# The first gate block of an encoder kernel from 32-bit products of unscaled rows, their norm applied behind

## The chip, the cores and the metric

The kernel runs on one core of a Trainium2 chip. The time is that of one execution on the device in microseconds, the median of several runs. TensorE (PE) multiplies, VectorE (DVE), ScalarE (ACT) and GpSimd (POOL) work on rows, and SyncE (SP) issues the DMAs. Each engine takes its instructions in the order in which they stand in its own queue.

## The reference

Two layers of an encoder over 2048 rows of 1024 numbers. Cut to what matters here:

```python
for l in range(DEPTH):                       # DEPTH = 2
    h = rmsnorm(x, pre_g[l])                 # x / sqrt(mean(x*x) + eps) * pre_g
    proj = h @ w_in[l]                       # (2048, 1024) @ (1024, 2816)
    u_a, v_a, g_a, q, k, v, g_b = split(proj)
    y_a = gmlp_group(u_a, v_a, ...) * silu(g_a)
    y_b = gqa_axial_attention(q, k, v, ...) * silu(g_b)      # g_b: 512 columns
    x = x + rmsnorm(concat(y_a, y_b) @ w_out[l], post_g[l])
```

The change concerns g_b of the first 512 rows in the first layer.

## The kernel before

The rows are worked on in four groups of 512 (`GRP`), each of four row blocks of 128. For a group, `hT_jobs` makes `hT`, the normalised rows turned so that the 1024 columns lie on the partitions, in two 16-bit halves: `load` brings a row block `x_t`, `squares` sums its squares on ACT, a chain of small steps on DVE (`chain`, `chain_two`; tiles `rs`, `rr`) makes the inverse norm, `scale` multiplies the left half of the row on ACT and the right half on POOL, `turn` transposes four 128x128 blocks on PE into a PSUM tile `pt` (a bundle, below), `high` casts that to the upper 16-bit half on ACT and `low` subtracts on DVE for the lower half. A weight block of 256 columns, `w_raw`, is split likewise by `split_steps`: maxima and a small product `pe` over all partitions give a power of two, then eight pieces are made into 16-bit halves `w_hl` (upper on ACT, lower on DVE), each multiplied by the gain `g_col` on the way. `proj_tok` then multiplies one row block by one weight block in three passes of eight 16-bit products (upper by upper, upper by lower, lower by upper), and `do_gb` makes the gate from two such results: tanh on ACT, one step on DVE, a store to `gb_d`.

The order of blocks begins with the two gate blocks `gb0` and `gb1` for group 0, then for groups 1, 2 and 3, then keys and the rest. Other work is hung into a block by `bg`, a list of jobs with due times: a `tick` comes after every pass of eight products, and jobs whose tick has come are issued there, at most four at a time. A gate block has 12 ticks, so the gates of group 1 start at tick 24, those of group 2 at tick 48. `start(g + 1)` hangs the next group's squares, norms and transposes in; for group 2 the transposes come at ticks 38 to 45. Engines named `PE`, `ACT`, `DVE`, `POOL` in capitals keep the program's order (`Pinned`, whose line 89 is that of nearly all instructions in the profile); the others are placed by the scheduler of the build.

Group 0 is opened by hand, at the end of the program: the first row block is loaded, squared, scaled, turned and split, the first weight is measured by squares on ACT (`sums=4`) and split on ACT, DVE and POOL, and the rest follows through `bg`:

```python
    z = jobs.chain(0)
    steps[1]()
    jobs.scale(0, z)
    steps[2]()
    banks = [jobs.turn(0, 0)]
...
    for d in range(ND):
        w.high(d, d % 2 == 1)
...
    for n, f in enumerate(steps2):
        bg.add((5, 5, 8, 9, 10, 10, 10, 10, 11, 11, 11, 11, 11)[n], f)
```

PSUM has eight banks for all tiles of `ps_t`; a tile's bank is taken again when its last reader is done.

Of the kernel before, what the change touches and what calls it, by code (L numbers as in the profile page):

```python
# [9 lines left out]
F32 = mybir.dt.float32  # L10
# [4 lines left out]
ALU = mybir.AluOpType  # L15
# [4 lines left out]
P = 128  # L20
# [23 lines left out]
def encoder(ctx: ExitStack, tc, x, w_in, w_out, pre_g, post_g, ln_a_g, ln_a_b,  # L44
# [19 lines left out]
    def big_t(shape, name, dt=F32R):  # L64
        return big.tile(shape, dt, name=name, tag="big")
# [4 lines left out]
    def f_t(name, n=GRP, dt=F32):  # L70
        return fp.tile([P, n], dt, name=name, tag="f")
# [4 lines left out]
    def ps_t(name):  # L76
        return psum.tile([P, GRP], F32, name=name, tag="ps", bufs=8)
# [66 lines left out]
            f()  # L144
        return z

    def rsqrt_rows_steps(parts, v, eps):

        n = parts.shape[1]
        m, z, t = [small.tile([P, n], F32, name=f"rr_{i}", bufs=2) for i in range(3)]  # L150
# [50 lines left out]
    class Project:  # L201
# [22 lines left out]
        def begin(self):  # L224

            self.w_first = [Obj(), Obj()]
            steps = []
# [123 lines left out]
        def split_steps(self, w, raw, act=ACT, dve=DVE, sums=0):  # L351

            w.ready = False
            col = small.tile([P, 32], F32, name="w_col", bufs=5)
# [2 lines left out]

            def part(i):
                sl = slice(i * ND // 2, (i + 1) * ND // 2)
                if i == 0 and sums:  # L360
                    def f():
                        for d in range(sums):
                            junk = f_t("fb")
                            act.activation(junk[:, 0:WB], raw[:, d], AF.Square, scale=self.g_col[:, d:d + 1],
                                           accum_out=col[:, 18 + d:19 + d])
                    return f
                return lambda: dve.tensor_reduce(top[:, sl], raw[:, sl], AX.X, ALU.max, apply_absolute_value=True)

            def square():
                ds8 = slice(sums, ND)  # L370
                dve.tensor_tensor(top[:, ds8], top[:, ds8], self.g_col[:, ds8], ALU.mult)
                dve.tensor_reduce(sq, top[:, ds8], AX.X, ALU.max, apply_absolute_value=True)
                if sums:
                    dve.tensor_reduce(inv, col[:, 18:18 + sums], AX.X, ALU.add)
                    dve.tensor_scalar(sq, sq, sq, inv, ALU.mult, ALU.add)
                    dve.tensor_scalar(sq, sq, W_SPREAD, None, ALU.mult)
                else:
                    dve.tensor_scalar(sq, sq, sq, W_SPREAD, ALU.mult, ALU.mult)

            def scale():  # L380
                ps = ps_t("pe")
                PE.matmul(ps[:, 0:1], ones, sq, start=True, stop=True)
                ei = w.e.bitcast(I32)
                dve.tensor_scalar(ei, ps[:, 0:1].bitcast(I32), -0.5, RSQRT_MAGIC, ALU.mult, ALU.add)
                dve.tensor_scalar(ei, ei, EXP_BITS, None, ALU.bitwise_and)
                dve.tensor_scalar(ei, ei, float(87 << 23), float(187 << 23), ALU.max, ALU.min)
                dve.tensor_scalar(w.eg, self.g_col, w.e, None, ALU.mult)

            def high(d, on_dve=False):
                if d == 0:  # L390
                    w.hl = w_t([P, 2, ND, WB], "w_hl", F16)
                if on_dve:
                    dve.tensor_scalar(w.hl[:, 0, d], raw[:, d], w.eg[:, d:d + 1], None, ALU.mult)
                    return
                act.activation(w.hl[:, 0, d], raw[:, d], AF.Copy, scale=w.eg[:, d:d + 1])

            def low(d, lo=None):
                if lo:
                    scaled = f_t("fb")[:, 0:WB]
                    lo.tensor_scalar(scaled, raw[:, d], w.eg[:, d:d + 1], None, ALU.mult)  # L400
                    lo.tensor_tensor(w.hl[:, 1, d], scaled, w.hl[:, 0, d], ALU.subtract)
                    return
# [32 lines left out]
        def hT_jobs(self, g):  # L435
# [61 lines left out]
            def trans(j, q):  # L497
# [43 lines left out]
        def norm_rope(self, banks, n, tb, eps):  # L541
# [10 lines left out]
            for i, src in enumerate(banks):  # L552
# [204 lines left out]
        def run(self, kv, first, last_jobs, first_wo):  # L757
# [168 lines left out]
    def attend(l, kv, nxt):  # L926
# [587 lines left out]
    jobs.squares(0)
    for j in range(1, TPG):
        jobs.load(j, ACT)
    steps[0]()
    z = jobs.chain(0)
    steps[1]()
    jobs.scale(0, z)  # L1520
    steps[2]()
    banks = [jobs.turn(0, 0)]
    jobs.squares(1)
    steps[3]()
    banks.append(jobs.turn(0, 1))
    jobs.high(0, 0, banks[0])
    w = pj.w_first[0]
    for d in range(ND):
        w.high(d, d % 2 == 1)
        if d == 2:  # L1530
            jobs.high(0, 1, banks[1])
    for q in range(2):
        jobs.low(0, q, banks[q])
    z = jobs.chain(1)
    for d in (ND - 2, ND - 1):
        w.low(d, POOL)
    jobs.squares(2)
    jobs.scale(1, z)
    jobs.squares(3)
    for d in range(ND - 2):  # L1540
        w.low(d)
    steps[12]()
    z2 = jobs.chain_two(2)
    for m, f in enumerate(trans[2:]):
        bg.add((2, 2, 4, 4, 7, 7)[m], f)
    for j in range(2):
        bg.add(2, lambda j=j: jobs.scale(2 + j, z2[:, j:j + 1]))
# [53 lines left out]
```

## Time and profile before

| what | value |
|---|---|
| runs | 2412.02, 2411.40, 2411.63 us, median 2411.63 |
| profiled execution | 2411.77 us, its span 2409.9 us |
| busy in the span | PE 98%, DVE 73%, ACT 68%, POOL 51% |
| PE idle in the first 45 us | 18.3 us |
| first gate product of group 0 | starts at 14.27 us |
| gates of group 1 (tick 24) | start at 53.57 us |

A row of the timeline gives start and duration in us, engine, line, operation, output and input tiles, shapes and count; behind it in brackets how long the engine was idle before and what released it. A row of the groups gives busy time and the mean duration of one in ns. In the table of stretches, each engine's busy us stands with its number of instructions, then the clock granted to PE and the DMA share.

### The profile page before, as it was taken

The numbers are of one execution on the slowest core, as the hardware profiler recorded it, in microseconds if no ns is written. First come the engines' busy times: TensorE is split into PE (matmuls) and PEld (weight loads), VectorE is DVE, ScalarE is ACT, GpSimd is POOL, SyncE is SP. The second block draws the span as 40 slices with busy tenths as digits, with TensorE's granted clock in tenths as the row PEclk, the third lists the DMA queues.
The fourth block names the chain that finished last, engine by engine and source line by source line (L and its number), as shares of the span: only waits on it lengthen the run. The fifth ranks groups of instructions, "written<-read, shape, count | busy, mean of one in ns | idle before, by whom it ended". The sixth has DMA issues, their size and how long they took to land. (4 is left out here: it accounts for less than half of the span.)

```text
span 2409.9 us, 62877 instructions
## 1 busy us (share of the span) xinstructions
PE 2365.5 (98%) x25327; PEld 1507.0 (63%) x25327; DVE 1755.6 (73%) x3979; ACT 1637.9 (68%) x3545; POOL 1235.4 (51%) x1022
## 2 busy tenths in 40 slices
PE   6999999999999999999999999999999999999997
PEld 5988776345555555555689887763455555555554
DVE  6668566866788888787776875678667777777774
ACT  6565323248898989888954742231588888888886
POOL 2200110026887888888821111100488888888886
PEclk9999999999999999999999999999999999999999
DMA  6352213222121222121153422222321121111110
GB/s 203 120 183 73 69 40 91 58 88 74 56 84 53 60 67 72 57 61 61 57 196 116 150 62 71 75 56 66 105 73 39 47 67 57 56 56 57 62 51 37
DMA packets 174917, 188.12 MB, mean 78 GB/s; under 512 B 19608, under 2 KB 143648, under 8 KB 174624
## 3 DMA queue, kind: packets, MB, share of 16 engines
q1 hardware_dynamic: 174192, 182.52, 24.9%
q8 instruction: 198, 3.24, 0.6%
q10 hardware_dynamic: 432, 1.57, 0.2%
q14 instruction: 95, 0.78, 0.1%
HBM read 129.38 MB, written 54.66 MB: 76 GB/s over the span
## 5 line engine op out<-in xcount | busy, mean ns | idle before, releaser
L89 POOL TENSOR_TENSOR p_parts<-p_f,p_parts 128x512 f16<-128x512 f32 x894 | 1077.8, 1219 | 250.9 <-ACT p_f L89 215.4
L89 ACT ACTIVATE p_parts<-sp 128x512 f16<-128x512 f32 x1024 | 623.4, 609 | 147.6 <-PE sp L89 74.2
L89 PEld LDWEIGHTS <-p_parts 128*128 128x128 f16 x12288 | 492.6, 97 | 286.8 <-issue 92.8
L89 ACT ACTIVATE p_f<-sp 128x512 f32<-128x512 f32 x1024 | 622.2, 608 | 0.0
L89 PE MATMUL pp<-w_hl,hT 128*128 128x256 f16 x5376 | 617.6, 274 | 4.5 <-ACT w_hl L89 4.1
L89 DVE TENSOR_REDUCE mx<-pmax 128x1 f32<-128x512 f32 x800 | 495.9, 681 | 112.5 <-PE pmax L89 112.0
L89 PEld LDWEIGHTS <-hT 128*128 128x128 f16 x5376 | 524.4, 98 | 72.1 <-issue 4.3
L89 PE MATMUL po<-v_st,p_parts 128*128 128x65 f16 (+1 forms) x12288 | 542.3, 193 | 2.7 <-POOL p_parts L89 1.8
L89 PE MATMUL pout<-wo,y_t 128*128 128x512 f16 x1536 | 463.0, 379 | 1.0 <-ACT y_t L89 0.5
L89 PE MATMUL sp<-q,k_t 66*128 66x512 f16 x1024 | 390.4, 381 | 0.0
L89 PE MATMUL sp<-q_st,k_t 128*128 128x512 f16 x1024 | 388.2, 379 | 1.9 <-ACT p_f L89 0.9
L89 PE MATMUL pp<-hT,w_hl 128*128 128x512 f16 x1536 | 347.6, 380 | 1.0 <-DVE mx L991 1.0
L89 PEld LDWEIGHTS <-w_hl 128*128 128x128 f16 x1536 | 145.0, 98 | 187.7 <-issue 26.6
L89 PEld LDWEIGHTS <-y_t 128*128 128x128 f16 x1536 | 150.4, 98 | 171.0 <-ACT y_t L89 0.7
L89 POOL TENSOR_TENSOR wo<-wo_raw,wo 128x512 f16<-128x512 f32 x32 | 37.0, 1156 | 255.3 <-ACT wo L89 253.6
L89 PE MATMUL pmax<-k_t,q_m 64*128 64x512 f16 x1024 | 164.0, 381 | 3.4 <-DVE mx L89 1.6
L991 DVE TENSOR_REDUCE mx<-pmax 128x1 f32<-128x512 f32 x224 | 140.5, 683 | 29.2 <-PE pmax L89 29.0
L638 POOL TENSOR_TENSOR fl<-fv,fh 128x512 f16<-128x512 f32 x32 | 37.9, 1205 | 206.6 <-ACT fh L637 197.9
L89 PEld LDWEIGHTS <-k_t 128*128 128x128 f16 (+1 forms) x2048 | 132.3, 97 | 5.6 <-issue 2.8
L89 DVE TENSOR_TENSOR p_parts<-p_f,p_parts 128x512 f16<-128x512 f32 x130 | 97.7, 752 | 42.3 <-ACT p_f L89 42.0
L538 POOL TENSOR_TENSOR fa<-fa,gain_q 128x512 f32<-128x512 f32 x16 | 20.7, 1294 | 190.6 <-DMA fa<-in_rope_dram 160.2
L556 ACT ACTIVATE fc<-pp,rs_y 128x64 f32<-128x64 f32 x320 | 69.8, 354 | 69.7 <-DVE rs_y L125 69.7
(216 smaller groups left out, 2097.1 us busy)
## 6 DMA issues: line engine op xcount, KB each, us to landing
w_raw<-in_w_in_dram SPq DMA_DIRECT2D x20, 512.0 KB
w_raw<-in_w_in_dram SPq DMA_DIRECT2D x10, 1024.0 KB
gb_d<-fa SPq DMA_DIRECT2D x32, 256.0 KB
wo_row<-in_w_out_dram SPq DMA_DIRECT2D x16, 512.0 KB
wo_raw<-in_w_out_dram SPq DMA_DIRECT2D x16, 512.0 KB
z_d<-fb SPq DMA_DIRECT2D x32, 256.0 KB
fb<-z_d SPq DMA_DIRECT2D x32, 256.0 KB
ya_d<-fa SPq DMA_DIRECT2D x32, 256.0 KB
```

Of the source, the lines that this page charges most:

```text
L89: return tc.keep_in_program_order(call(*args, **kw))
L538: nc.gpsimd.tensor_tensor(cs, cs, gain.unsqueeze(1).broadcast_to([P, TPG, 2, HD]), ALU.mult)
L556: nc.scalar.activation(qn[:, t, h], src[:, t, h], AF.Copy, scale=rs[:, i, t, h:h + 1])
L638: nc.gpsimd.tensor_tensor(s.lo, vh, s.hi, ALU.subtract)
L991: dve.tensor_reduce(s.mx[:, j, c:c + 1], pm[c], AX.X, ALU.max)
```

## The change

In layer 0 the two gate blocks of group 0 no longer wait for a norm or for 16-bit halves. The rows of group 0 are turned as they were loaded and copied from PSUM into `h32`, a 32-bit tile (`open_turn`; in the lists of instructions below its name is shortened to `h_145`). The gate weights are multiplied by the gain in place on DVE (`open_weight`), and `open_block` multiplies `h32` by `w_raw` as 32-bit numbers, eight products for a row block and a weight. The four inverse norms are made in one chain (`open_norm`) and enter the gate twice: as the scale of the tanh (`z_half`, in `open_gate`), and as a factor `ze` in the finish of attention for the first four row blocks. The 16-bit halves of group 0's rows, which keys and all later blocks use, are made afterwards from `h32`: `open_spread` (tick 28) puts each norm on a diagonal on DVE and multiplies it by ones on PE, so that `z_row` holds the norm of every row on every partition; eight `open_split` (ticks 31, 33, ... 45) multiply a piece of `h32` by `z_row` on POOL, cast it on ACT and subtract on POOL. The weights are still split for groups 1 to 3, with their maxima on DVE alone (`plain`), at ticks 4 to 26. The row blocks 1 to 3 are loaded by SP ahead of the second weight, not by ACT's queue behind it.

```diff
-                steps.append(([load], self.split_steps(w, raw, sums=4)))
+                self.w_raw.append(raw)
+                steps.append(([load], self.split_steps(w, raw, plain=True)))
...
+        def open_turn(self, j):
+            for q in range(2):
+                ps = self.jobs0.turn(j, q)
+                dst = self.h32[:, 4 * q:4 * q + 4, j * P:(j + 1) * P]
+                if j == 0 and q == 1:
+                    DVE.tensor_copy(dst, ps)
+                else:
+                    ACT.copy(dst, ps)
+        def open_weight(self, n, d):
+            raw = self.w_raw[n]
+            DVE.tensor_scalar(raw[:, d], raw[:, d], self.g_col[:, d:d + 1], None, ALU.mult)
...
+        def open_spread(self):
+            ps = ps_t("pz")
+            for j in range(TPG):
+                diag = f_t("fb")[:, 0:P]
+                DVE.tensor_scalar(diag, ident, self.z4[:, j:j + 1], None, ALU.mult)
+                PE.matmul(ps[:, j * P:(j + 1) * P], ones, diag, start=True, stop=True)
+            self.z_row = f_t("z_row")
+            ACT.copy(self.z_row, ps)
+        def open_split(self, d):
+            h, hT = self.h32[:, d], self.first
+            POOL.tensor_tensor(h, h, self.z_row, ALU.mult)
+            ACT.copy(hT[:, 0, d], h)
+            POOL.tensor_tensor(hT[:, 1, d], h, hT[:, 0, d], ALU.subtract)
...
+        def open_block(self, n):
...
+                for d in range(ND):
+                    PE.matmul(ps, self.h32[:, d, j * P:(j + 1) * P], self.w_raw[n][:, d, :],
+                              start=d == 0, stop=d == ND - 1)
+                    if d == 3 and n == 0 and j + 1 < TPG:
+                        self.open_turn(j + 1)
+                        self.jobs0.squares(j + 1)
+                    if d in (2, 5, 7):
+                        bg.tick()
...
+                if l == 0 and t < TPG:
+                    DVE.tensor_scalar(s.rd, s.rd, pj.ze[:, t, kv:kv + 1], None, ALU.mult)
...
+    bg.add(9, pj.open_norm)
+    for n, f in enumerate(steps):
+        bg.add((4, 5, 9, 10, 11, 12, 13, 14, 15, 16, 17, 18, 18)[n], f)
     for n, f in enumerate(steps2):
-        bg.add((5, 5, 8, 9, 10, 10, 10, 10, 11, 11, 11, 11, 11)[n], f)
+        bg.add((13, 14, 15, 17, 19, 20, 21, 22, 23, 24, 25, 26, 26)[n], f)
+    bg.add(28, pj.open_spread)
+    for d in range(ND):
+        bg.add(31 + 2 * d, lambda d=d: pj.open_split(d))
```

What moves in the queues shows at three places. First DVE, around the start of group 1's gates, before: the low halves of group 1's rows (`hT<-pt,hT`), the gates (`fa`), the maxima of the key weight (`w_col<-w_raw`), and then the norm chain of group 2.

```order
L89 TENSOR_TENSOR hT<-pt,hT 128x4x128 x3
L677 SCALAR_TENSOR_TENSOR fa<-fa,pp 128x512
L89 TENSOR_TENSOR hT<-pt,hT 128x4x128 x2
L89 TENSOR_REDUCE w_col<-w_raw 128x4 x2
L89 TENSOR_TENSOR w_col<-w_col,g_col 128x8
L89 TENSOR_REDUCE w_col<-w_col 128x1
L89 TENSOR_SCALAR w_col<-w_col 128x1
L89 SCALAR_TENSOR_TENSOR rr_801<-ss_x 128x2
```

The same place on DVE now; `fb<-ident,z_146` are the four diagonals for which PE's products `pz` wait:

```order
L89 TENSOR_TENSOR hT<-pt,hT 128x4x128 x2
L89 TENSOR_REDUCE w_col<-w_raw 128x4 x2
L89 TENSOR_TENSOR w_col<-w_col,g_col 128x8
L89 TENSOR_REDUCE w_col<-w_col 128x1
L89 TENSOR_SCALAR w_col<-w_col 128x1
L89 SCALAR_TENSOR_TENSOR w_hl<-w_raw,w_col,w_hl 128x256
L89 SCALAR_TENSOR_TENSOR fa<-fa,pp 128x512
L89 SCALAR_TENSOR_TENSOR w_hl<-w_raw,w_col,w_hl 128x256
L89 TENSOR_SCALAR w_col<-w_col 128x1 x5
L89 TENSOR_SCALAR fb<-ident,z_146 128x128 x4
```

The last lower halves of the second gate weight, a gate and the diagonals now stand between the key weight's maxima and the norm chain of group 2. Second POOL, before, from the scalings of group 0's last row blocks to those of group 2 (`rr_801` and `rr_849` are group 2's norms, `rr_802` and `rr_850` their results):

```order
L89 TENSOR_SCALAR x_t<-x_t,rr_266 128x512 x2
L89 TENSOR_SCALAR x_t<-x_t,rr_497 128x512 x2
L89 TENSOR_SCALAR x_t<-x_t,rr_554 128x512 x2
L89 TENSOR_SCALAR x_t<-x_t,rr_802 128x512 x2
L89 TENSOR_SCALAR x_t<-x_t,rr_850 128x512 x2
```

POOL now, from group 1's last scalings on; `rr_654` and `rr_705` are group 2's norms:

```order
L89 TENSOR_SCALAR x_t<-x_t,rr_396 128x512 x2
L89 TENSOR_TENSOR h_145<-h_145,z_row 128x512
L89 TENSOR_TENSOR hT<-h_145,hT 128x512
L89 TENSOR_SCALAR x_t<-x_t,rr_654 128x512 x2
L89 TENSOR_TENSOR h_145<-h_145,z_row 128x512
L89 TENSOR_TENSOR hT<-h_145,hT 128x512
L89 TENSOR_SCALAR x_t<-x_t,rr_705 128x512 x2
L89 TENSOR_TENSOR h_145<-h_145,z_row 128x512
```

Group 2's scalings now stand behind the first and the second of the eight pairs, and six pairs follow them. Third ACT, before, at group 2's transposes (`hT<-pt`):

```order
L89 ACTIVATE x_t<-x_t,rr_850 128x512 x2
L89 CAST hT<-pt 128x4x128 x2
L89 ACTIVATE w_hl<-w_raw,w_col 128x256
L89 CAST hT<-pt 128x4x128
L89 ACTIVATE w_hl<-w_raw,w_col 128x256
L89 CAST hT<-pt 128x4x128
L89 ACTIVATE w_hl<-w_raw,w_col 128x256
```

ACT now, at the same place; `hT<-h_145` are the casts of the pairs:

```order
L89 ACTIVATE x_t<-x_t,rr_705 128x512 x2
L89 CAST hT<-h_145 128x512 x2
L89 CAST hT<-pt 128x4x128
L749 ACTIVATE fa<-pp,w_col 128x512
L89 CAST hT<-h_145 128x512
L89 CAST hT<-pt 128x4x128
L89 ACTIVATE w_hl<-w_raw,w_col 128x256
L89 CAST hT<-pt 128x4x128
L89 CAST hT<-h_145 128x512
```

Two casts that wait for POOL's products now stand ahead of group 2's first cast, and one ahead of nearly every second cast behind it.

More of the change, by code (lines that the diff above doesn't have):

```diff
@@ L145, in rsqrt_rows, with rsqrt_rows_steps @@
         return z
-    def rsqrt_rows_steps(parts, v, eps):
+    def rsqrt_rows_steps(parts, v, eps, tag=""):
         n = parts.shape[1]
-        m, z, t = [small.tile([P, n], F32, name=f"rr_{i}", bufs=2) for i in range(3)]
+        m, z, t = [small.tile([P, n], F32, name=f"rr{tag}_{i}", bufs=2) for i in range(3)]
         steps = [lambda: v.scalar_tensor_tensor(m, parts[:, :, 0], eps, parts[:, :, 1], ALU.add, ALU.add),
@@ L226, in begin @@
             self.w_first = [Obj(), Obj()]
+            self.w_raw = []
             steps = []
@@ L349, in fill_w, with split_steps @@
                                   w_in[self.l, :, c:c + n].rearrange("(d p) e -> p d e", p=P))
-        def split_steps(self, w, raw, act=ACT, dve=DVE, sums=0):
+        def split_steps(self, w, raw, act=ACT, dve=DVE, plain=False):
             w.ready = False
@@ L359, in part @@
                 sl = slice(i * ND // 2, (i + 1) * ND // 2)
[L360 to L366, printed above, removed]
                 return lambda: dve.tensor_reduce(top[:, sl], raw[:, sl], AX.X, ALU.max, apply_absolute_value=True)
             def square():
[L370 to L378, printed above, removed]
+                if not plain:
+                    dve.tensor_tensor(top, top, self.g_col, ALU.mult)
+                dve.tensor_reduce(sq, top, AX.X, ALU.max, apply_absolute_value=True)
+                dve.tensor_scalar(sq, sq, sq, W_SPREAD, ALU.mult, ALU.mult)
             def scale():
@@ L386, in scale, with factor @@
                 dve.tensor_scalar(ei, ei, float(87 << 23), float(187 << 23), ALU.max, ALU.min)
-                dve.tensor_scalar(w.eg, self.g_col, w.e, None, ALU.mult)
+                if not plain:
+                    dve.tensor_scalar(w.eg, self.g_col, w.e, None, ALU.mult)
+            def factor(d):
+                return w.e if plain else w.eg[:, d:d + 1]
             def high(d, on_dve=False):
@@ L503, in hT_jobs @@
             jobs = Obj()
+            jobs.parts = parts
             jobs.load, jobs.squares, jobs.one, jobs.two, jobs.turn, jobs.done = load, squares, one, two, turn, done
@@ L565, in norm_rope, with open_rows @@
             return outs
+        def open_rows(self, jobs):
+            self.h32 = big_t([P, ND, GRP], "h32", F32)
+            self.z4 = lay.tile([P, TPG], F32, name="z4")
+            self.z_half = lay.tile([P, TPG], F32, name="z_half")
+            self.ze = lay.tile([P, TPG, 2], F32, name="ze")
+            self.jobs0 = jobs
+        def open_turn(self, j):
[6 more added lines that the diff above has]
+                    ACT.copy(dst, ps)
@@ new lines, in open_weight, with open_norm @@
+        def open_weight(self, n, d):
+            raw = self.w_raw[n]
+            DVE.tensor_scalar(raw[:, d], raw[:, d], self.g_col[:, d:d + 1], None, ALU.mult)
+        def open_norm(self):
+            z, steps = rsqrt_rows_steps(self.jobs0.parts, DVE, D * EPS, "4")
+            for f in steps:
+                f()
+            DVE.tensor_copy(self.z4, z)
+            DVE.tensor_scalar(self.z_half, z, 0.5 / NORM_SCALE, None, ALU.mult)
+        def open_spread(self):
[6 more added lines that the diff above has]
+            ACT.copy(self.z_row, ps)
@@ new lines, in open_split @@
+        def open_split(self, d):
[3 more added lines that the diff above has]
+            POOL.tensor_tensor(hT[:, 1, d], h, hT[:, 0, d], ALU.subtract)
+            if d == ND - 1:
+                turned[id(hT)] = {(j, q) for j in range(TPG) for q in range(2)}
+        def open_block(self, n):
+            banks = []
+            for j in range(TPG):
+                if j % 2 == 0:
+                    banks.append(ps_t("pp"))
+                ps = banks[-1][:, (j % 2) * WB:(j % 2 + 1) * WB]
+                for d in range(ND):
[6 more added lines that the diff above has]
+                        bg.tick()
+                if j % 2:
+                    bg.add(max(1, 10 - bg.now), lambda i=j // 2: self.open_gate(n, i, banks[i]))
@@ L567, in banked, with open_gate @@
+        def open_gate(self, n, i, ps):
+            th = f_t("fa")
+            for t in range(2):
+                sl = slice(t * WB, (t + 1) * WB)
+                ACT.activation(th[:, sl], ps[:, sl], AF.Tanh, scale=self.z_half[:, 2 * i + t:2 * i + t + 1])
+            DVE.scalar_tensor_tensor(th, th, 1.0, ps, ALU.add, ALU.mult)
+            nc.sync.dma_start(gb_d[0][:, 2 * i:2 * i + 2, n * WB:(n + 1) * WB],
+                              th.rearrange("p (t e) -> p t e", t=2))
         def banked(self, hT, w):
@@ L805, in block @@
             def block(name, g):
+                if self.l == 0 and g == 0 and name in ("gb0", "gb1"):
+                    self.open_block(int(name[2]))
+                    self.opening = False
+                    return
                 assert all(w[n].ready for n in (("va0", "va1") if name == "va" else (name,)))
@@ L1504, in encoder @@
     pj = layers[0]
-    pj.first, trans, jobs = pj.hT_jobs(0)
+    pj.first, _, jobs = pj.hT_jobs(0)
+    pj.open_rows(jobs)
     jobs.load(0)
@@ L1510, in encoder @@
     loads[0](1)
+    for j in range(1, TPG):
+        jobs.load(j)
     loads2[0](0)
@@ L1513, in encoder @@
     pj.norm_turn()
+    pj.open_turn(0)
     jobs.squares(0)
[L1515 to L1527, printed above, removed]
-    for d in range(ND):
[L1529 to L1547, printed above, removed]
+    for d in range(ND):
+        pj.open_weight(0, d)
+    for n in range(4):
+        for d in range(2):
+            bg.add(5 + n, lambda d=2 * n + d: pj.open_weight(1, d))
+    bg.add(9, pj.open_norm)
+    for n, f in enumerate(steps):
+        bg.add((4, 5, 9, 10, 11, 12, 13, 14, 15, 16, 17, 18, 18)[n], f)
     for n, f in enumerate(steps2):
-        bg.add((5, 5, 8, 9, 10, 10, 10, 10, 11, 11, 11, 11, 11)[n], f)
+        bg.add((13, 14, 15, 17, 19, 20, 21, 22, 23, 24, 25, 26, 26)[n], f)
+    bg.add(28, pj.open_spread)
+    for d in range(ND):
+        bg.add(31 + 2 * d, lambda d=d: pj.open_split(d))
     for l in range(DEPTH):
```

10 lines of the change are left out of this document (6 added, 4 removed).

## The prediction

> **What bounds the kernel now.** I read the page first: its busy shares and its slices in time.
>
> ```profile
> PE 2365.5 (98%) x25327; PEld 1507.0 (63%) x25327; DVE 1755.6 (73%) x3979; ACT 1637.9 (68%) x3545; POOL 1235.4 (51%) x1022
> PE   6999999999999999999999999999999999999997
> ```
>
> PE is the bound nearly everywhere, so a change can gain only where PE is not full, the first slice. The table of stretches dates it.
>
> ```profile
> core 0: us, PE busy (x) PEld busy (x) DVE busy (x) ACT busy (x) POOL busy (x), PEclk, DMA share, GB/s
> 0.00:15.00 15.00, 3.42 (x15) 2.52 (x15) 7.16 (x26) 8.52 (x23) 3.34 (x8) 1.00 0.88 306
> 15.00:30.00 15.00, 11.30 (x69) 8.21 (x68) 11.60 (x36) 10.35 (x27) 7.05 (x6) 0.89 0.64 195
> 30.00:45.00 15.00, 12.01 (x103) 9.84 (x102) 10.65 (x42) 11.09 (x30) 0.87 (x1) 1.00 0.44 140
> 45.00:60.00 15.00, 15.00 (x139) 13.77 (x138) 12.34 (x36) 10.37 (x22) 5.33 (x4) 1.00 0.58 176
> 90.00:105.00 15.00, 15.00 (x140) 13.82 (x138) 12.22 (x43) 11.61 (x26) 7.27 (x4) 1.00 0.36 106
> ```
>
> PE loses 18.3 us of the first 45 (15.00 less its busy time, three rows) and nothing after; there DVE stands at 12.3 of 15 us. So DVE has little to spare, and whatever PE loses past 45 us nothing returns. The timeline of PE gives the places that I compare (start, duration, count):
>
> ```profile
> 9.70 1.12 PE L89 MATMUL pt<-ident,x_t 128*128 128x128 f32 x4 [5.21 <-ACT x_t L89]
> 14.27 1.01 PE L89 MATMUL pp<-w_hl,hT 128*128 128x256 f16 x4 [2.12 <-ACT w_hl L89]
> 15.54 2.72 PE L89 MATMUL pp<-w_hl,hT 128*128 128x256 f16 x12 [0.27 <-ACT w_hl L89]
> 18.61 0.66 PE L89 MATMUL pt<-ident,x_t 128*128 128x128 f32 x4 [0.34 <-ACT x_t L89]
> ...
> 24.45 0.66 PE L89 MATMUL pt<-ident,x_t 128*128 128x128 f32 x4 [1.92 <-ACT x_t L89]
> ...
> 46.15 0.60 PE L89 MATMUL pt<-ident,x_t 128*128 128x128 f32 x4
> 46.59 1.04 PE L89 MATMUL pp<-w_hl,hT 128*128 128x256 f16 x8
> ...
> 53.57 6.60 PE L89 MATMUL pp<-w_hl,hT 128*128 128x256 f16 x59
> ...
> 73.84 0.60 PE L89 MATMUL pt<-ident,x_t 128*128 128x128 f32 x4
> ...
> 90.57 0.64 PE L89 MATMUL pt<-ident,x_t 128*128 128x128 f32 x4
> ...
> 153.12 1.09 PE L89 MATMUL pt<-wsT,fb 128*64 128x128 f32 x16
> ```
>
> At 53.57 the gates of group 1 begin; 73.84 is the seventh bundle of transposes for group 2, 90.57 the first for group 3. A bundle of four takes 0.44 (46.15 to 46.59), a 16-bit product 0.108 (15.00/139).
>
> **Unknown price: a 32-bit product of 256 columns.** The 32-bit products of L89 `pt<-wsT` (8 of them, two records each, half the array's columns) took 1.09: 0.136 for 128 columns, 0.27 for 256, the lower end. A 32-bit transpose, which fills the array and has one record, takes 0.11 for 128 columns; two records and two times 128 columns make 0.44, the upper end. I take 0.43, nearest to the row that fills the array.
>
> [...]
>
> **Prices of the other engines.** From the timeline and the groups:
>
> ```profile
> 4.53 0.17 DVE L89 COPY g_col<-pt 128x8 f32<-128x8 f32 x1 [3.54 <-PE pt L89]
> 12.07 1.29 DVE L89 TENSOR_SCALAR w_hl<-w_raw,w_col 128x256 f16<-128x256 f32 x3
> ...
> 37.80 0.69 DVE L677 SCALAR_TENSOR_TENSOR fa<-fa,pp 128x512 f32<-128x512 f32 x1 [0.70 <-ACT fa L676]
> 38.81 1.68 DVE L89 SCALAR_TENSOR_TENSOR w_hl<-w_raw,w_col,w_hl 128x256 f16<-128x256 f32 x4 [0.32 <-ACT w_hl L89]
> 40.41 0.64 DVE L89 TENSOR_SCALAR w_col<-w_col 128x1 int32<-128x1 int32 x5
> 41.84 0.16 DVE L89 SCALAR_TENSOR_TENSOR rr<-ss_x 128x2 f32<-128x2 f32 x1 [0.80 <-ACT sq L89]
> ...
> 43.81 0.16 DVE L89 SCALAR_TENSOR_TENSOR rr<-rr,rr 128x2 f32<-128x2 f32 x1
> ...
> 51.10 0.34 DVE L89 TENSOR_REDUCE g_top<-gain_k 128x1 f32<-128x64 f32 x2
> ...
> 52.44 0.28 DVE L89 TENSOR_SCALAR gain_q<-gain_q,g_exp 128x128 f32<-128x128 f32 x1
> ...
> 55.02 1.28 DVE L89 TENSOR_TENSOR hT<-pt,hT 128x512 f16<-128x512 f32 x2
> 56.22 2.34 DVE L89 TENSOR_REDUCE w_col<-w_raw 128x4 f32<-128x1024 f32 x2
> ```
>
> ```profile
> 38.28 1.69 ACT L89 ACTIVATE w_hl<-w_raw,w_col 128x256 f16<-128x256 f32 x4
> ...
> 41.10 0.58 ACT L89 ACTIVATE sq<-x_t 128x512 f32<-128x512 f32 x1
> ...
> 41.72 0.58 ACT L89 ACTIVATE sq<-x_t 128x512 f32<-128x512 f32 x1
> ...
> 44.01 1.33 ACT L89 ACTIVATE x_t<-x_t,rr 128x512 f32<-128x512 f32 x2 [0.22 <-DVE rr L89]
> ...
> 49.16 2.15 ACT L89 CAST hT<-pt 128x512 f16<-128x512 f32 x4
> ```
>
> ```profile
> 61.59 3.10 POOL L89 TENSOR_SCALAR x_t<-x_t,rr 128x512 f32<-128x512 f32 x2 [11.26 <-DVE rr L89]
> ```
>
> ```profile
> L538 POOL TENSOR_TENSOR fa<-fa,gain_q 128x512 f32<-128x512 f32 x16 | 20.7, 1294 | 190.6 <-DMA fa<-in_rope_dram 160.2
> L638 POOL TENSOR_TENSOR fl<-fv,fh 128x512 f16<-128x512 f32 x32 | 37.9, 1205 | 206.6 <-ACT fh L637 197.9
> ```
>
> DVE: low half of a weight piece 0.42, small step 0.13 to 0.2, gate 0.66, a norm chain 2.13 (41.84 to 43.97), low half of rows 0.64, maximum of half a weight 1.2, gains 1.5 (51.10 to 52.6). ACT: high half 0.42, row block squared 1.24 (two at 0.62), half row block scaled 0.66, cast 0.54. POOL: row scaled 1.55, product 1.29, difference 1.2. Engines hand over in about 0.06.
>
> **Leg 1, up to the spread of the norms.** Gained: no norm, no scaling and no halves before the first product. Transposes can start behind g_col's (4.7); eight at the slow rate of 9.70 take 2.2, DVE's copy 0.65, one weight piece 0.4: first product at about 7.7, against 14.27 before. Then 20 products and five bundles stand ahead of row block 3's copies: 8.6 + 2.2, plus about 2 while PE is still slow, to 20.4. Before, PE ran at half rate from 9.70 (a bundle 1.12, later 0.66) until 18.3, over some 6 us of work; with fewer gaps here I let it end at 11.6.
>
> Then a chain: ACT copies twice and squares (1.1 + 1.2, 22.8), DVE makes the norm and the weight's square (2.1 + 0.9, 25.9), PE's one-column product waits 2.1 for it. From 26.3 DVE has, before the four diagonals that PE's spread needs: 16 low halves of weights 6.7, two chains 4.3, four gates 2.6, four maxima 4.8, eight low halves of rows 5.1, gains 1.5, small steps 4.4, diagonals 0.8: 30.2. It also waits 5.1 for ACT, since each pair of chains sends ACT to scale two blocks (1.33) before the next high half (0.42), and the first gates come late. Sum 26.3 + 35.3 = 61.6. Added on DVE are 16 weight scalings (cheap: DVE waits for x there); moved onto these 35 us are both weights' low halves, which before were partly done at the start on POOL and ahead of 45.
>
> PE comes to the spread far earlier: 44 more products (18.9), nine more bundles (4.0) and two one-column products (0.6), with waits of 2.1 and 4.5 for the squares of the two weights (DVE reaches the second only at 38.8), end at 50.4 (before 53.57), and 32 16-bit products at 53.9. There it waits 7 us, and all of group 1 waits behind it. The spread, four products of 0.22, ends at 61.9 (the first diagonals are ready before the last); before, this place was at 53.57 + 3.45 = 57.0. Leg 1: **+4.9 us**, though the opening itself is 3 us earlier.
>
> **Leg 2, ticks 28 to 48.** z_row's copy ends at 62.6. POOL now has eight pairs of 1.29 + 1.2 with ACT's cast between (0.65 with hand-overs), about 3.1 each, and group 2's four row scalings (6.2) among them, in one queue. ACT's casts stand in ACT's own queue ahead of group 2's casts of transposes. In order: pair 0 until 67.4 (ACT is still squaring, 1.8 late), two scalings to 71.1, pair 1 to 74.2, a wait until 77.2 for the next chain (its squares stood behind pair 1's cast on ACT), scalings to 80.3, pair 2 to 83.4, product 3 and its cast to 85.3. Only then ACT casts group 2's first transpose, DVE takes its low half: 86.5. All eight PSUM banks are taken by then (six transposes, two gates), so PE's seventh bundle waits about 6 us for that: 86.5 against 73.84. Leg 2 brings it to **+12.7 us**.
>
> **Leg 3, group 3's norms.** The remaining casts alternate with POOL's pairs (four at 3.1 from 85.3: 97.2 + 1.5), so DVE's last low half ends at 99.4. Behind it on DVE: two weight pieces 0.9, two gates 1.3, small steps 0.6 + 0.8, four maxima 4.8, a chain with other small steps between 2.7: 110.5; ACT scales 0.66: PE's first transpose for group 3 at 111.3 against 90.57. That is +20.7; the next chain costs 1.8 more. **Sum: +22.** Eight extra small steps in attention hang on nothing that PE waits for: 0. The profiled execution took 2411.77 (span 2409.9 + 1.9), 0.14 over the median; 2411.8 + 22 = **2434 us**.
>
> **Rivals.** (a) Faster: DVE keeps up, for which only its idle third of the first 15 us speaks. Then PE's waits of 2.1, 4.5 and 7 vanish, 50.4 becomes 43.8 against 53.57, with 0.9 more for the spread: −8.9, 2403. It decides if DVE's diagonals are done by 47.3, 14 us sooner than summed; 0.09. (b) Pairs hide: leg 1 alone, 2416.7, if ACT casts transposes without waiting for POOL; its queue speaks against it; 0.13. (c) DVE catches up before group 3: legs 1 and 2, 2424.5; 0.17. (d) More than that: PE's clock falls at each wait as below, and DVE and POOL slow one another: +28, 2440; 0.12.
>
> ```profile
> 26.00:27.00 1.00, 1.00 (x7) 0.75 (x6) 0.45 (x1) 0.43 (x1) 0.90 (x1) 0.50 0.00 0
> ```
>
> After PE's gap of 1.92 us ahead of 24.45 the granted clock was 0.50. The loss after the first two waits is covered by the next wait; after the third, about 1.5 us are not.
>
> [...]
>
> (e) Leg 1 alone and the low price of a product, 2413.7: within 0.2%; 0.05.
>
> **Numbers.** My forecast holds 0.44. At the low price of a product leg 1 shrinks by 20 times 0.16, 3 us, since DVE sets the rest. Range 2415 to 2443: from (b) to just past (d); left out are (a), (e) and a little above. A difference of 0.2% (4.8 us) is about what a measurement can tell: faster 0.09, same 0.07 (with a little of (b)), slower 0.84.
>
> **What would show it.** Right: `pp<-w_raw` from about 8 us; PE idle before `pz` released by DVE near 61; PE's transposes near 80 waiting for ACT or DVE while `hT<-h32` casts wait for POOL; group 3's transposes near 111. Wrong: `pz` met without a wait, or POOL pairs under 2 us.

## The result and the profile after

The changed kernel took 2436.14 us (median of four runs, 2435.11 to 2437.11), the kernel before 2411.82 beside it: a ratio of 1.0099 with an interval of 1.0086 to 1.0111, 24 us slower. The forecast was 2434. The profiled execution has a span of 2433.3 us, 23.4 more than before. One execution of a run below, that with the cast on POOL, took 3019.97 us at a clock of 0.752 and is left out of its median.

The page again: busy shares, and PE in 40 slices. PE is busier than before and the kernel is longer; the second slice, full before, is now at 7.

```profile
PE 2382.1 (98%) x25271; PEld 1521.5 (63%) x25271; DVE 1758.4 (72%) x3980; ACT 1637.5 (67%) x3541; POOL 1249.1 (51%) x1030
PE   7799999999999999999999999999999999999997
```

The table of stretches, with the columns as before:

```profile
0.00:15.00 15.00, 9.64 (x35) 8.16 (x36) 5.51 (x15) 5.72 (x12) 0.70 (x6) 1.00 0.87 301
...
45.00:60.00 15.00, 11.49 (x81) 9.95 (x79) 14.69 (x44) 8.47 (x19) 0.00 (x0) 1.00 0.51 158
...
75.00:90.00 15.00, 8.08 (x65) 6.76 (x63) 3.86 (x18) 5.73 (x13) 9.99 (x8) 0.83 0.32 95
...
105.00:120.00 15.00, 9.09 (x63) 7.60 (x62) 9.89 (x44) 7.31 (x17) 4.22 (x3) 0.77 0.34 102
```

In the first 15 us PE is busy for 6.2 us more than before: the opening does what it says. Then come three holes where PE had been full: at 45 to 60 (DVE full, 14.69 of 15), at 75 to 90 (DVE idle, POOL the busiest), at 105 to 120. PE's timeline shows what stands behind each:

```profile
7.50 3.75 PE L89 MATMUL pp<-w_raw,h 128*128 128x256 f32 x8 [1.09 <-DVE w_raw L89]
...
17.33 3.62 PE L89 MATMUL pp<-w_raw,h 128*128 128x256 f32 x16
20.79 1.04 PE L89 MATMUL pt<-ident,x_t 128*128 128x128 f32 x8
...
26.77 0.43 PE L89 MATMUL pe<-w_col,ones 128*128 128x1 f32 x2 [1.92 <-DVE w_col L89]
...
39.55 0.38 PE L89 MATMUL pe<-w_col,ones 128*128 128x1 f32 x2 [2.43 <-DVE w_col L89]
...
52.83 3.66 PE L89 MATMUL pp<-w_hl,hT 128*128 128x256 f16 x32
60.59 1.64 PE L89 MATMUL pz<-fb,ones 128*128 128x128 f32 x8 [4.10 <-DVE fb L89]
62.02 10.09 PE L89 MATMUL pp<-w_hl,hT 128*128 128x256 f16 x80
71.95 0.28 PE L89 MATMUL pe<-w_col,ones 128*128 128x1 f32 x2
...
88.17 1.11 PE L89 MATMUL pt<-ident,x_t 128*128 128x128 f32 x4 [5.79 <-DVE hT L89]
...
109.42 0.56 PE L89 MATMUL pe<-w_col,ones 128*128 128x1 f32 x2 [3.58 <-DVE w_col L366]
112.19 1.11 PE L89 MATMUL pt<-ident,x_t 128*128 128x128 f32 x4 [2.21 <-ACT x_t L89]
...
123.42 0.60 PE L89 MATMUL pt<-ident,x_t 128*128 128x128 f32 x4
```

The spread ends at 62.02 (PE was past that place of group 1's gates at 57.0 before), group 2's seventh bundle starts at 88.17 (73.84), group 3's first at 112.19 (90.57) and its last at 123.42 (99.78): 23.6 late, and so it stays to the end. The one-column products `pe` ahead of the transposes of groups 2 and 3 (71.95 and 109.42) are also places to compare. Before:

```profile
65.80 0.28 PE L89 MATMUL pe<-w_col,ones 128*128 128x1 f32 x2
...
90.43 0.28 PE L89 MATMUL pe<-w_col,ones 128*128 128x1 f32 x2
```

The row at 88.17 names DVE; the queues of POOL, ACT and DVE ahead of it name the first cause:

```profile
81.89 1.26 POOL L89 TENSOR_TENSOR h<-h,z_row 128x512 f32<-128x512 f32 x1
...
84.99 1.26 POOL L89 TENSOR_TENSOR h<-h,z_row 128x512 f32<-128x512 f32 x1
```

```profile
86.28 0.62 ACT L89 CAST hT<-h 128x512 f16<-128x512 f32 x1 [2.48 <-POOL h L89]
86.81 0.58 ACT L89 CAST hT<-pt 128x512 f16<-128x512 f32 x1
```

```profile
87.42 0.69 DVE L89 TENSOR_TENSOR hT<-pt,hT 128x512 f16<-128x512 f32 x1 [8.70 <-ACT hT L89]
```

DVE had idled 8.70 us for ACT's first cast of group 2 (86.81), which stood behind the cast of pair 3 (86.28), which had waited 2.48 for POOL. A pair's period on POOL is 3.10 us (81.89 to 84.99), and up to 3.38 among the later pairs.

### The profile page after: what moved, and what is told of

Same layout as the page of the kernel before. It is cut to its first block, busy times and chain, and to the rows that moved or that the text cites. A ratio compares the mean times of both kernels' runs of the same rounds, so it can differ in the third digit from the quotient of the medians.

```text
span 2433.3 us, 62743 instructions
## 1 busy us (share of the span) xinstructions
PE 2382.1 (98%) x25271; PEld 1521.5 (63%) x25271; DVE 1758.4 (72%) x3980; ACT 1637.5 (67%) x3541; POOL 1249.1 (51%) x1030
## 5 line engine op out<-in xcount | busy, mean ns | idle before, releaser
L89 PE MATMUL pp<-w_hl,hT 128*128 128x256 f16 x5184 | 594.8, 274 | 0.0
L89 PEld LDWEIGHTS <-hT 128*128 128x128 f16 x5184 | 507.0, 98 | 63.9 <-issue 0.8
```

What stands on the lines that cost most here:

```text
L89: return tc.keep_in_program_order(call(*args, **kw))
```

## The experiments

Each ratio is to the kernel before, measured together with the run (2411.8 to 2412.9 us). Two questions: does the loss come from where the new work stands, or from the work; and are the three legs separate causes?

**The last four splits later.**

```diff
-        bg.add(31 + 2 * d, lambda d=d: pj.open_split(d))
+        bg.add(31 + 2 * d if d < 4 else 67 + 3 * (d - 4), lambda d=d: pj.open_split(d))
```

> Of the eight splits the first four stay at ticks 31 to 37, the last four go to ticks 67 to 76. This parts leg 2 from leg 3. Queue theory: leg 2 stays, since group 2's first cast stands behind the fourth pair in ACT's queue as in the changed kernel: its seventh bundle near 88 us, its eighth near 92 (17 us behind the 75.15 of before). Behind it no cast waits for POOL, ACT and DVE end group 2's halves some 6 us earlier (near 96 instead of 102.8), and PE's waits of 3.58 and 2.21 us ahead of group 3 go: 2411.8 + 17 = 2429 (2427 to 2431). Rival 'leg 3 is only leg 2 carried on' (DVE is late because group 2 came late): 2435 to 2437. Rival 'the last four make all of it' (the first four hide): 2420 or less.

Measured: 2430.58 us, 1.0076 (1.0063 to 1.0090). PE's timeline:

```profile
87.73 1.12 PE L89 MATMUL pt<-ident,x_t 128*128 128x128 f32 x4 [4.23 <-DVE hT L89]
...
107.47 0.63 PE L89 MATMUL pt<-ident,x_t 128*128 128x128 f32 x4
```

Leg 2 is there as before (87.73), leg 3's waits are gone: group 3's first bundle has no bracket. So leg 3 hangs on the last four splits, and is not leg 2 carried on. The run takes their casts from ACT's queue and their products from POOL together; which of the two matters, it does not tell.

**All splits later, the spread at its place.**

```diff
-        bg.add(31 + 2 * d, lambda d=d: pj.open_split(d))
+        bg.add(67 + 3 * d, lambda d=d: pj.open_split(d))
```

> The spread stays at tick 28, only the eight splits go to ticks 67 to 88. Queue theory: leg 1 stays as it is (the last product of the spread at 62.0 against 57.0 at that place before, +5), legs 2 and 3 vanish, since no cast of ACT waits for POOL ahead of groups 2 and 3: 2416.9 (2415 to 2419). Rival 'one backlog' (legs 2 and 3 are leg 1 carried on by DVE): 2425 or more. Rival 'legs do not add' (PE would have waited for the norms of group 2 anyway): 2421 to 2425.

Measured: 2419.65 us, 1.0032 (1.0020 to 1.0044).

```profile
62.28 9.46 PE L89 MATMUL pp<-w_hl,hT 128*128 128x256 f16 x80
...
96.36 0.63 PE L89 MATMUL pt<-ident,x_t 128*128 128x128 f32 x4
```

Leg 1 is unchanged (62.28), and group 2's bundles have no wait: legs 2 and 3 come from the splits, not from leg 1. The number lies 0.65 above the expected range: group 3's first bundle is 5.8 late, and a wait of 0.54 among its bundles and later ones add to that. Differences of the ratios give the legs in time: about 7.7 us with leg 1 alone, 18.3 with legs 1 and 2, 23.9 with all; so 7.7, 10.6 and 5.6. The interval of each ratio reaches about 3 us to both sides, and late splits bring small waits of their own, so these sizes are rough; the changed kernel's own trace gives others below.

**DVE relieved ahead of the spread.**

```diff
-                        before(lambda: bg.add(20, lambda: self.scale_gains(DVE)))
+                        before(lambda: bg.add(52, lambda: self.scale_gains(DVE)))
...
-            for f in steps[:3]:
-                f()
+            if pinned and self.l == 0 and bg.now < 30:
+                bg.add(5, lambda: [f() for f in steps[:3]])
+            else:
+                for f in steps[:3]:
+                    f()
```

> Two things that DVE does ahead of the four diagonals go behind them, nothing else: the maxima of the key weight with their two small steps (2.8 us, from tick 24 to 29) and the gains (1.4 us, from tick 20 to 52). PE's order is unchanged. Queue theory: DVE sets the spread, so it comes 4.2 us earlier (last product at about 57.8), PE's wait ahead of it is about gone, and as POOL's pairs start from it, everything behind comes earlier by about the same: 2432 (2430.5 to 2434). Rival 'POOL and ACT set it' (the chain of pairs and group 2's norms decide, the spread only fills a wait): less than 1 us, 2435 to 2437. Rival 'moved, not removed' (the 4.2 us come back ahead of group 2's low halves): 2436.

Measured: 2432.06 us, 1.0085 (1.0072 to 1.0098), 4.1 less than the changed kernel's 2436.14, or 3.4 by the ratios.

```profile
56.43 1.13 PE L89 MATMUL pz<-fb,ones 128*128 128x128 f32 x8 [0.33 <-DVE fb L89]
```

PE's wait is 0.33 instead of 4.10. Taking 4.2 us from DVE took 3 to 4 from the end: DVE's queue sets leg 1, and POOL's pairs start from it (the first at 58.27 instead of 62.93). In the profiled execution group 2's seventh bundle is 5.1 earlier (83.07) and group 3's last only 2.8 (120.61), so a part came back at group 3, as the third rival had it.

**PE's two early waits moved.** If DVE sets the spread, they cost nothing.

```diff
-        bg.add((4, 5, 9, 10, 11, 12, 13, 14, 15, 16, 17, 18, 18)[n], f)
+        bg.add((4, 5, 9, 12, 12, 12, 13, 14, 15, 16, 17, 18, 18)[n], f)
...
-        bg.add((13, 14, 15, 17, 19, 20, 21, 22, 23, 24, 25, 26, 26)[n], f)
+        bg.add((13, 14, 15, 19, 20, 20, 21, 22, 23, 24, 25, 26, 26)[n], f)
```

> The changed kernel with the two one-column products of the gate weights (and the pieces behind them that would come before them) two ticks later: tick 12 instead of 10, 19 instead of 17. PE no longer stands before them for DVE's squares (1.92 and 2.43 us). Queue theory: nothing is gained, since DVE sets the spread and has the same work ahead of it; PE's wait ahead of the spread grows by what the two waits give back: 2436 (2434.5 to 2437.5). Rival 'each wait is a loss of its own': 4.4 us less, 2431.5.

Measured: 2435.27 us, 1.0095 (1.0081 to 1.0109).

```profile
38.87 0.38 PE L89 MATMUL pe<-w_col,ones 128*128 128x1 f32 x2 [2.96 <-DVE w_col L89]
59.92 2.05 PE L89 MATMUL pz<-fb,ones 128*128 128x128 f32 x8 [8.37 <-DVE fb L89]
```

The first wait went, the second did not (2.96), and PE arrived earlier to wait 8.37 us at the spread, which ended where it had (61.76). So the early wait cost nothing here: DVE set the spread, and PE only waited there longer.

**The cast moved from ACT to POOL.**

```diff
-            ACT.copy(hT[:, 0, d], h)
+            POOL.tensor_copy(hT[:, 0, d], h)
```

> In each split the cast of the upper half goes from ACT to POOL, so ACT's queue no longer holds anything that waits for POOL; POOL has three steps a pair, about 3.6 us, and no hand-over. Queue theory: group 2's casts run as soon as PE has turned the rows, its seventh bundle comes at about 82 instead of 88 and leg 2 shrinks by 6; group 3's scalings stand on POOL behind the last split, which now ends at about 104 (81.9 + 6 x 3.6), so its first bundle from POOL comes at about 105 against 91.9 before: +13, 2425 (2421 to 2429). Rival 'POOL is the bound' (any more work on POOL makes it later, whatever ACT's queue holds): 2436 to 2446. Rival 'ACT's queue was all': 2417.

Measured: 2426.77 us, 1.0060 (1.0047 to 1.0073).

```profile
80.98 1.27 POOL L89 TENSOR_TENSOR h<-h,z_row 128x512 f32<-128x512 f32 x1
82.32 0.68 POOL L89 CAST hT<-h 128x512 f16<-128x512 f32 x1
83.08 1.17 POOL L89 TENSOR_TENSOR hT<-h,hT 128x512 f16<-128x512 f32 x1
...
102.74 3.11 POOL L89 TENSOR_SCALAR x_t<-x_t,rr 128x512 f32<-128x512 f32 x2 [2.04 <-DVE rr L89]
```

PE has no wait left in group 2's bundles, so the 5.79 us at 88.17 came through ACT's queue, not from POOL's speed. The way to the number was partly wrong: a cast took POOL 0.61 to 0.69 us, a pair 3.1 to 3.4 and not 3.6, and group 3's scalings waited for DVE's norm (2.04), not for the last split.

Leg 3 did not go with the casts. PE is ready for the one-column product ahead of group 3 at 97.48 (99.65 less a wait of 2.17), 7.05 behind the 90.43 of before, and starts group 3's last bundle at 114.67, 14.89 behind: 7.8 are lost in between. DVE's rows show one cause, its low halves of the weight while POOL makes pairs:

```profile
89.86 2.86 DVE L89 SCALAR_TENSOR_TENSOR w_hl<-w_raw,w_col,w_hl 128x256 f16<-128x256 f32 x2
```

These two took 2.86 instead of twice 0.42. All eight took 9.4 us here, 6.3 in the changed kernel, and 3.7 with the last four splits late, where POOL was idle.

**The x loads put back behind the second weight.**

```diff
-    for j in range(1, TPG):
-        jobs.load(j)
     loads2[0](0)
     loads2[0](1)
...
     jobs.squares(0)
+    for j in range(1, TPG):
+        jobs.load(j, ACT)
```

> The changed kernel with one part undone: row blocks 1 to 3 are loaded by ACT's queue behind the second weight's issue, as before, not by SP ahead of it. Queue theory: they come about 1 MB later (2.7 us at the 390 GB/s of that stretch), PE waits for them in the opening, the squares of row block 3 end 3 to 6 us later, and as the chain of norms starts DVE's long queue ahead of the spread, all of it comes as much later: 2440 (2438 to 2443). Rival 'loads are hidden' (DVE's and PE's own waits cover them): 2435 to 2437.

Measured: 2441.73 us, 1.0119 (1.0106 to 1.0133).

```profile
26.72 1.06 PE L89 MATMUL pt<-ident,x_t 128*128 128x128 f32 x8 [1.30 <-DMA x_t<-in_x_dram]
...
66.49 2.04 PE L89 MATMUL pz<-fb,ones 128*128 128x128 f32 x8 [5.79 <-DVE fb L89]
```

Row block 3 is turned 5.9 us later and the spread comes as much later. This part of the change was worth 5.6 us, or 4.8 by the ratios.

**Spread and splits late.** Can the loss be had back?

```diff
-    bg.add(28, pj.open_spread)
+    bg.add(64, pj.open_spread)
...
-        bg.add(31 + 2 * d, lambda d=d: pj.open_split(d))
+        bg.add(67 + 3 * d, lambda d=d: pj.open_split(d))
```

> Only the place changes: the spread of the norms at tick 64 instead of 28, the eight splits at ticks 67 to 88 instead of 31 to 45. Queue theory (that of the prediction: the loss comes from what stands in DVE's, POOL's and ACT's queues ahead of groups 1, 2 and 3): the three legs vanish together, PE has no wait between 55 and 122 us, group 3's first transposes start within 2 us of the 90.57 of before, 2412 us (2409 to 2414). Rival 'work': PE's 32-bit products cost it 64 x 0.433 - 192 x 0.108 = 7 us more than the 16-bit ones, and these are lost wherever the splits stand: 2418 to 2420. Rival 'backlog': DVE is behind by its own work, and a wait removed at one place comes back at the next: group 2's seventh bundle stays 5 us or more behind the 73.84 of before, 2420 or more.

Measured: 2418.78 us, 1.0031 (1.0019 to 1.0043).

```profile
89.44 0.63 PE L89 MATMUL pt<-ident,x_t 128*128 128x128 f32 x4
...
96.02 1.63 PE L89 MATMUL pz<-fb,ones 128*128 128x128 f32 x8 [3.76 <-DVE fb L89]
```

The number is that of the rival 'work', the place is not: group 3's first bundle comes 1.1 us before 90.57, and the loss is a new wait at tick 64, where the diagonals stand on DVE behind group 3's low halves. Place alone gave back some 17 of the 24 us. The next run moved spread and splits again, and gave every second split's two steps to DVE:

```diff
+            eng = DVE if d % 2 else POOL
...
+    bg.add(74, pj.open_spread)
...
+        bg.add(76 + 2 * d, lambda d=d: pj.open_split(d))
```

> Only the place again, chosen by the run with the spread at 64, where the four diagonals stood in DVE's queue behind group 3's low halves and PE waited 3.76 us for them: now the spread at tick 74 and the splits at ticks 76 to 90, every second one's two steps on DVE instead of POOL, so that they end before the keys at tick 96. Queue theory: the waits for the two weights stay (1.92 and 4.04 in that run), none follows, group 3's last transposes start within 1.5 us of the 99.78 of before: 2412 (2410 to 2414). Rival 'work' (7 us more of PE for 32-bit products are lost wherever the rest stands): 2417 to 2420. Rival 'keys wait' (the splits end behind tick 96): 2416 or more.

Measured: 2415.51 us, 1.0011 (1.0002 to 1.0020). The waits of PE in the first 130 us (what it waited for: us in total, times, longest):

```profile
PE pe L89 <- DVE w_col L89: 6.0, 2, 4.0
PE pt L89 <- ACT x_t L89: 1.0, 2, 0.8
PE pz L89 <- DVE fb L89: 0.8, 1, 0.8
```

Place, together with the pairs shared between POOL and DVE, gives back all but about 3 us of the 24. The run lies between the ranges of all three expectations. In the profiled execution the 2412 expected was missed by small waits of which the two longest are 0.81 (1.8 in all), the spread's own products (0.9) and a first product at 8.53 instead of 7.50; that start lay anywhere from 7.50 to 8.59 in the runs that leave the loads alone.

**Versions meant to keep the opening's gain.** With the run just told, the second weight's low halves on POOL, the products of the weights later, the key weight's maxima (`steps[:3]`) and the gains behind:

```diff
+                    low(d, on_pool)
...
+                bg.add(5, lambda: [f() for f in steps[:3]])
...
+                        before(lambda: bg.add(52, lambda: self.scale_gains(DVE)))
...
+        bg.add((4, 5, 9, 12, 12, 12, 13, 14, 15, 16, 17, 18, 18)[n], f)
...
+        bg.add((13, 14, 15, 21, 22, 22, 23, 23, 24, 25, 26, 27, 27)[n], f)
```

> The kernel of the run with the spread at 74, and DVE relieved in the opening: the one-column products at ticks 12 and 21, the second weight's low halves on POOL (two steps each) instead of DVE, the key weight's maxima at tick 29, the gains at tick 52. Queue theory: both early waits of PE go (1.9 and 4.0 us, with the slower clock behind them about 6.5), nothing takes their place, group 3's last transposes start at about 94: 2406 (2404 to 2409), faster than before. Rival 'backlog' (PE now comes 6 us earlier to the transposes and gates of group 1, where DVE and ACT are not ready): 2410 to 2413.

Measured: 2415.95 us, 1.0014 (1.0005 to 1.0022).

```profile
48.76 12.28 PE L89 MATMUL pp<-w_hl,hT 128*128 128x256 f16 x111
...
70.15 0.66 PE L89 MATMUL pt<-ident,x_t 128*128 128x128 f32 x4 [1.84 <-ACT x_t L89]
...
97.27 0.66 PE L89 MATMUL pt<-ident,x_t 128*128 128x128 f32 x4 [1.84 <-ACT x_t L89]
```

The rival 'backlog' was right in kind, too low in its number: PE waits already among group 1's transposes (0.55 and 2.07), still leads by 4.8 us at group 1's gates, and loses that to norms of groups 2 and 3 that are not ready (twice 1.84), to POOL's last low half of the second weight (1.03) and to the spread (a wait of 1.04 and its products).

Then the norms of groups 2 and 3 two ticks earlier, the maxima behind both chains of group 2, more low halves on POOL, the gains at tick 78:

```diff
+                bg.add(11, lambda: [f() for f in steps[:3]])
...
-                k = 5 if early else 0
+                k = 5 if early else (-2 if self.l == 0 else 0)
...
+    bg.add(77, pj.open_spread)
...
+        bg.add(79 + 2 * d, lambda d=d: pj.open_split(d))
```

> What the two last runs showed to be next is moved as well. In the run with DVE relieved, PE was 4.8 us ahead of the kernel before at the gates of group 1 (48.76 against 53.57) and lost it again in four waits of 1.0 to 1.84 us, because the second pair of norms of groups 2 and 3 stood on DVE behind a gate, and behind POOL's last low halves of the second weight. Now: squares and norms of groups 2 and 3 two ticks earlier, the key weight's maxima behind both of group 2's chains (tick 35, its split two ticks later), the first weight's low halves and every second one of the second weight on POOL, the gains at tick 78, the spread at 77 and the splits at 79 to 93. Queue theory: the lead of about 5 us is kept, less 0.9 for the spread's products and under 1 for small waits: 2408 (2405 to 2410), faster than before. Rival 'backlog' (DVE and ACT have no more to give, another wait takes the place): 2412 to 2416.

Measured: 2420.21 us, 1.0036 (1.0022 to 1.0051), worse: the lead was 7.4 us, and then PE waited for the maxima that I had moved, and again 2.52 us at 130.61.

```profile
66.89 0.58 PE L89 MATMUL pe<-w_col,ones 128*128 128x1 f32 x2 [5.18 <-DVE w_col L89]
```

Two neighbours mended that (maxima at tick 30, spread at 76, splits from 77, three of them on POOL); the second leaves group 3's ticks alone.

> The run before led by 7.4 us at group 1's gates (46.17 against 53.57) and lost it in two waits that its own moves had made: 5.18 us for the key weight's maxima (now behind the second chain on DVE, ahead of a product of tick 40) and 2.52 us for the last halves ahead of the keys, both with a slower clock behind them. Now the maxima at tick 30, between group 2's two chains, where DVE waited 4.1 us for ACT; the spread at 76 and the splits at 77 to 91, with three on POOL and five on DVE. Queue theory: both waits go, about 10 us with the clock: 2410 (2407 to 2413), by 0.1% faster than before. Rival 'backlog': another wait takes their place, 2414 to 2418.

> As its neighbour, but group 3's squares and norms stay at their old ticks, only group 2's are earlier: the gate of tick 60 then stands ahead of group 3's second chain on DVE again. Queue theory: the wait of 0.97 us for that gate goes, the one of 0.8 to 1.84 us for the second chain comes back: within 1.5 us of its neighbour, 2410.5 (2407 to 2413). Rival 'backlog': 2414 to 2418.

Measured: 2413.63 us, 1.0007 (0.9998 to 1.0016), and 2412.05 us, 0.9999 (0.9990 to 1.0008). The first lies 0.6 above its range, the second inside it, but the gain that both were to show is not there: the second, the best of all, is level with the kernel before. Of its PE timeline:

```profile
48.49 1.80 PE L89 MATMUL pp<-w_hl,hT 128*128 128x256 f16 x15
...
68.94 1.03 PE L89 MATMUL pp<-w_hl,hT 128*128 128x256 f16 x8 [1.25 <-DVE fa L755]
...
94.88 0.66 PE L89 MATMUL pt<-ident,x_t 128*128 128x128 f32 x4 [1.59 <-ACT x_t L89]
...
153.47 1.09 PE L89 MATMUL pt<-wsT,fb 128*64 128x128 f32 x16
```

A lead of 5.1 us at the gates (48.49 against 53.57) is gone at 153.47 (153.12 before): group 2's gate and group 3's norms take 1.25 and 1.59 of it, the spread's products 0.9, waits below 0.4 a part of the rest. Whether DVE and ACT could be ordered so that it stays was not settled.

## Why the prediction was right

**The price of a product: right.** Two records are one product here: 16 records from 17.33 to 20.79, 3.46 us for 8, are 0.4325 each, against 0.43 taken, near the upper of the two bounds (0.44). It is 4.0 times the 0.108 of a 16-bit product.

**Leg 1: right up to the spread.** First product 7.50 (7.7 forecast), row block 3's first bundle over at 21.2 (20.4), the weights' products at 26.77 and 39.55 (26.0, 38.9), spread's end 62.02 (61.9). The join at group 1's gates was 2.4 late (52.83 against 50.4): 0.65 because DVE reached the second weight's squares that late, the rest because PE ran at half clock after the second wait (0.78, 0.50, 0.50 and 0.51 in the four us from 40 to 44, 1.7 us lost). It cost nothing, since the wait at the spread was that much shorter (4.10, not 7). Relieving DVE and moving the early wait both confirm that DVE set this leg. Behind the spread PE ran at half clock once more (0.52, 0.50, 0.50 and 0.77 in the four us from 61 to 65, 1.7 us lost), and the product at 71.95 is 6.1 late (65.80 before), not 4.9.

**Leg 2: mechanism right, size too small.** The seventh bundle came at 88.17, 1.7 later than forecast, by the named chain: POOL's pair, ACT's cast, group 2's first cast, DVE's low half. These 1.7 stand already at group 2's first scalings, with which POOL was done at 72.78, not 71.1: the norm's chain began late (66.49) and took 3.1 us, not 2.13, as one small step took 1.05 us beside a subtraction on POOL (last section). What the sum left out, and gave to rival (d), is the clock behind the wait. Stretches of 1 us, columns as above (the clock is the third number from the end):

```profile
84.00:85.00 1.00, 0.00 (x0) 0.00 (x0) 0.00 (x0) 0.00 (x0) 1.00 (x2) 0.97 0.00 0
...
90.00:91.00 1.00, 1.00 (x7) 0.67 (x6) 0.47 (x1) 1.00 (x4) 0.91 (x1) 0.50 0.84 184
91.00:92.00 1.00, 1.00 (x7) 0.76 (x6) 1.00 (x3) 0.38 (x1) 1.00 (x2) 0.62 0.89 250
```

From the bundle at 88.17 to about 91.8 PE works at half rate, 1.8 us lost. PE was ready for the product of 109.42 at 105.84, 15.4 behind the 90.43 of before: so much are legs 1 and 2 together, not 12.7.

**Leg 3: place right, cause in part, size somewhat too large.** Group 3's first bundle was forecast at 111.3 and came at 112.19, since DVE's queue sets it, but by two errors that partly cancel: DVE's last low half of rows ended at 102.1 (99.4 forecast), and what stands behind it took 9.3 and not 11.1. From 15.4 late to 23.6 late leg 3 adds 8.2 us in the changed kernel, not 9 to 10. The 5.6 from the ratios is smaller because, in the run with the last four splits late, half clock behind the wait lasted until about 93.8 (0.50 from 87 to 93 us, 0.59 in the next) and group 3 began 16.9 late (107.47), not 15.4. The prediction let DVE come late because ACT's casts alternate with POOL's pairs; but with these casts on POOL the leg was still 7.8. DVE's own steps that take longer while POOL makes pairs are the cause that the rows show; no run takes it away alone.

**The number: in part luck.** Legs 1 and 2 were 2.7 us larger than forecast, leg 3 some 1 to 2 smaller: +23.4 in the span against +22. The sum has two slips as well: four pairs of 3.1 from 85.3 end at 97.7, not 97.2, and 20.7 + 1.8 is 22.5; without them it would have been 23. The term put at nothing, the extra steps in attention, is borne out: PE is 23.6 late at 123.42 and the span ends 23.4 later.

**The rivals.** (a) did not come: DVE did not keep up. (b) needed ACT's casts free of POOL; with all splits late they were, and gave 2419.65, not 2416.7. (c) did not come either: DVE had not caught up before group 3, and PE waited there for 3.58 and 2.21 us. (d) named two things that both show in the rows, the clock at each wait and DVE and POOL slowing one another, and gave them too much: 2440. The estimate of 1.5 us behind the third wait has the size of the loss of before behind the gap ahead of 24.45: the clock was 0.67, 0.50, 0.50 and 0.62 in the four us from 25 to 29, 1.7 us lost. Behind the third wait of the changed kernel it was 1.7 as well, and half clock cost PE time behind the waits of the other two legs too (0.50 from 88 to 91 and from 109 to 115 us).

## What to carry to other kernels

Work taken out of a critical opening has to be done later, and there its place in the in-order queues counts for more than its amount: here 24 us were lost at one place, 7 at another, and some 3 at a third with half of the pairs on another engine. Before moving work, follow whose queue it stands in and who waits for what stands behind it; a cast on ACT that waits for POOL holds up everything that ACT has for PE (here a wait of ACT of 2.48 us, and 5.79 us of PE). An engine that takes over a step may also make another engine's steps longer, here POOL those of DVE (eight low halves of a weight took 6.3 us beside its pairs, 3.7 where POOL was idle). And once PE leads by 5 us, the next chain that had been hidden, here the norms (a wait of 1.59 us in the last run), takes the lead back.

## What was unexpected of the hardware

A wait of 1.92 us ahead of the same product was followed by half clock in the changed kernel (0.50 from 27 to 30 us) and by full clock in the run with the spread at 64 (1.00 from 26 to 34), so its length alone doesn't decide. Stretches of 1 us, first the changed kernel, then that run:

```profile
28.00:29.00 1.00, 1.00 (x4) 0.76 (x3) 1.00 (x3) 0.97 (x4) 0.00 (x0) 0.50 0.66 226
```

```profile
28.00:29.00 1.00, 1.00 (x6) 0.87 (x6) 0.26 (x1) 0.97 (x4) 0.00 (x0) 1.00 0.49 167
```

Worked out from such stretches (0.96 from 26 to 27 us puts the step from 1.00 to 0.50 at 26.92), the clock of the changed kernel changed at 26.92, 30.32, 40.56, 43.98, 61.04, 64.46, 84.94, 91.76, 108.84 and 115.66 us, each a whole number of times 3.413 us from the first to within 0.02 (115.66 less 26.92 is 26 times 3.413). What makes it change, no run here shows.

Steps of DVE and POOL took longer beside one another. In the norm's chain of group 2, on DVE, the step `rr<-rr,rr` takes 0.16 us further on (68.64); beside POOL's subtraction it took 1.05 and ended with it:

```profile
67.16 1.05 DVE L89 TENSOR_TENSOR rr<-rr,rr 128x2 f32<-128x2 f32 x1
```

```profile
67.04 1.15 POOL L89 TENSOR_TENSOR hT<-h,hT 128x512 f16<-128x512 f32 x1 [2.85 <-ACT hT L89]
```

Before, POOL had no subtraction there, and the same step took 0.16 (59.78). POOL's products in the changed kernel took 1.26 at 81.89 and 84.99, and 1.45 to 1.54 from 91.20 on, where DVE made low halves beside them.
